# A two-layer mixture-of-experts kernel: four experts in place in layer 1, smaller first blocks, second blocks under a branch

## The chip, the cores and the metric

The kernel runs on one core of a Trainium2 chip. A core has five engines that run side by side, each through its own list of instructions in order: TensorE (PE in the profile; PEld is its weight load), VectorE (DVE), ScalarE (ACT), GpSimd (POOL) and SyncE (SP), which here only issues transfers. Sixteen DMA engines move data between HBM and the core's memory. The metric is the time of one execution in device microseconds (us); less is better.

## The reference

256 latent tokens and 256 context tokens of width 1024 pass two layers. Layer 0 mixes tokens with a bidirectional recurrence (RG-LRU), layer 1 with attention; behind each stands a mixture of experts, over all 512 tokens in layer 0 and over the 256 latent ones in layer 1. Everything is fp32. The mixture, which is what the change is about, is:

```
def grouped_moe(h, router_w, router_b, w1, w3, w2):
    logits = (h @ router_w).astype(jnp.float32) + router_b.astype(jnp.float32)
    probs = jax.nn.softmax(logits, axis=-1)
    pg = probs.reshape(probs.shape[:-1] + (N_EXPERT_GROUPS, EXPERTS_PER_GROUP))
    group_score = lax.top_k(pg, TOP_K)[0].sum(-1)
    sel = jnp.argmax(group_score, axis=-1)
    ...
    top_w, top_i = lax.top_k(masked, TOP_K)
    top_w = top_w / jnp.sum(top_w, axis=-1, keepdims=True)
    gates = jnp.sum(jax.nn.one_hot(top_i, N_EXPERTS, dtype=jnp.float32) * top_w[..., None], axis=-2).astype(h.dtype)
    y = jnp.zeros_like(h)
    for e in range(N_EXPERTS):
        y = y + gates[..., e:e + 1] * ((jax.nn.silu(h @ w1[e]) * (h @ w3[e])) @ w2[e])
    return y
```

There are 16 experts in four groups of four; each token goes to two experts of one group. `w1` and `w3` are 1024 x 512, `w2` is 512 x 1024: 2 MB each, 6 MB an expert.

How many tokens an expert gets follows from the inputs. For the inputs of these runs the counts of rows are, with the experts that stand in place by their number and the others sorted:

| | in place | by rank, from the most to the fewest |
|---|---|---|
| layer 0, both kernels | 14, 27, 62 | 183, 125, 90, 73, 73, 66, 63, 51, 47, 43, 41, 40, 26 |
| layer 1, before | 11, 25, 52 | 147, 147, 32, 29, 26, 19, 16, 7, 1, 0, 0, 0, 0 |
| layer 1, changed | 11, 25, 52, 26 | 147, 147, 32, 29, 19, 16, 7, 1, 0, 0, 0, 0 |

## The kernel before, in words

**Weights.** Every weight of the two layers passes through one pool of 2 MB tiles named `w`. A list of jobs (`moe_jobs` for the experts) gives the order; `send` takes the next job, opens a tile and issues two 1 MB halves on SP's queue (L149), with at most four halves in flight. A tile is opened when an older one is given back (`done`), so TensorE's progress releases loads.

**Places.** Experts are worked through in 16 places. The first `FIRST` = 3 places are the experts 0 to 2, fixed, so that their weights load before the router has spoken. From place 3 on a place takes the expert of a certain rank (`ORDERS`), and its weights can go out only when the counts are known: `order()` (L1017 to L1038) sorts the counts and writes the expert numbers `eok`; SP reads them with a register load (L134) and waits there. Jobs stand in the order `w1` of place e, `w3` of place e, `w2` of place e-1; only at the places named by `TAIL` does `w2` come first. In layer 1 `TAIL` is 12: the places 12 to 15 run only if they have tokens, which they have not here.

**Rooms.** A place with a rank gathers as many rows as `ROOM` says, in blocks of 128, 64 or 32 rows; 160 is 128 and 32, 96 is 64 and 32 packed. A place of the first three has 64 rows (`BASE`) and, under a branch on its count, 128 more. Rows beyond the room would go to `leftover()`, which is skipped here.

**One step** e of `run`: `ups(e)` multiplies the gathered rows by `w1` and `w3` (L935), ScalarE takes silu (L939), VectorE the product (L940), and the next place's rows are turned (`turn`, L917). Then `downs(e-1)` multiplies by `w2` (L967), VectorE scales by the gates into `y` (L978 in layer 0, L975 in layer 1), and POOL adds the rows to `yr` or to the output by a scatter transfer (L981), each waiting for the one before. Then `flips(e)` transposes what `downs(e)` will need (L947 on TensorE, copied by VectorE at L949). A branch on the number of rows stands in `ups` (L1136), in `downs` (L1152) and in the gathers (L1009), each for the engines that have work in it.

**The end of layer 0.** Layer 1 begins under layer 0's last experts: its second `qkv` tile is converted by ScalarE (`wkv`, L1320), and the low parts are taken by VectorE and POOL in turn (`wkvl`, L1321). SP reads `yr` back when all scatters are down (L1349), and the gains and residuals follow (L1356, L1359). The order of instructions on each engine is set by a scheduler when the kernel is built; a branch closes a block, and work behind it can't move ahead of it.

Of the kernel before, what the change touches and what calls it, by code (L numbers as in the profile page):

```python
# [13 lines left out]
ALU = mybir.AluOpType  # L14
# [19 lines left out]
FIRST = 3  # L34
# [14 lines left out]
C_E = 212  # L49
C_KEY = 228  # L50
C_RANK = 244
C_ROOM = 276
C_N = 308

C_LT, C_IO, C_DUP = 308, 436, 692

C_COS, C_SIN = 1076, 1204
C_ALL = 1332
# [5 lines left out]

def room(i, k):
    return MORE if k < FIRST else ROOM[i][ORDERS[i][k - FIRST]]


def blocks(i, k):

    if k < FIRST:
        return [(KIND[BASE], 0)]
    r = room(i, k)
    return [(KIND[r], 0)] if r <= 128 else [(0, 0), (KIND[r - 128], 128)]
# [3 lines left out]
def hybrid_kernel(ctx: ExitStack, tc: tile.TileContext, x, c, ctxt, c_ctx, ada_w, ada_b, norm_mix_w, norm_ffn_w,  # L78
# [39 lines left out]
    def send(pool=wp):  # L118
# [10 lines left out]
        if key[0] in ("w1", "w2", "w3") and key[2] >= FIRST:  # L129
# [65 lines left out]
    def moe_jobs(i):  # L195
        for e in range(E):
            names = [("w1", moe_w1, 0), ("w3", moe_w3, 0), ("w2", moe_w2, 1)]
            for name, w, d in names[2:] + names[:2] if e in (TAIL[i], TAIL[i] + 2) else names:
                for k in [e - d] + ([e] if d and e == E - 1 else []):
                    if 0 <= k < FIRST:  # L200
                        add_job((name, i, k), [(0, 4096, w[i, k].rearrange("(k p) f -> p k f", p=128))])
                    elif k >= FIRST:
# [522 lines left out]
    def moe_(R, rp, early):  # L725
# [17 lines left out]
        with tc.tile_pool(reuse_waits="tile", name=f"r{i}", bufs=1) as q:  # L743
            V = rp.tile([128, C, E, NV], BF16, name="V")
            cg = cst[:, C_CG:C_CG + C * E].rearrange("p (c e) -> p c e", c=C)
# [77 lines left out]
            def gates():  # L823
# [3 lines left out]
                values(0, FIRST, gate)  # L827
# [14 lines left out]
        class Lists:  # L842
# [5 lines left out]
            def match(self):  # L848
# [34 lines left out]
            def expand(self):  # L883
                m, w = self.nb, self.nb * NV
                px = mbank("pa", 1) if self.e >= FIRST or self.left else mbank("py", 2)
# [114 lines left out]
        def fetch_next(e):  # L1000
# [13 lines left out]
        def order():  # L1014

            key = rp.tile([128, E], F32, name="key")
            nc.vector.scalar_tensor_tensor(key, cnf, 16.0, cst[:, C_KEY:C_KEY + E], ALU.mult, ALU.add)  # L1017
# [48 lines left out]
        def lists(e):  # L1066
            bases = [0, BASE] if e < FIRST else [at for _, at in blocks(i, e)]
# [9 lines left out]
        def load_n(e):  # L1077
            return nc.values_load((cn if e < FIRST else counts[i][0])[0:1, e:e + 1], engines=main, min_val=0, max_val=T)
# [632 lines left out]
```

## Time and profile before

| | |
|---|---|
| three runs | 991.46, 989.19, 991.61 us; median 991.46 |
| the profiled execution | 988.14 us, of which the span of the trace is 986.1 |
| TensorE busy in the span | 860.8 us, 87%; mean granted clock 0.946 |
| VectorE, ScalarE, POOL busy | 489.9, 302.6, 252.1 us |
| moved by DMA | 277.00 MB, mean 281 GB/s |
| chain that ended last | DMA 21%, PE 11%, VectorE 6% of the span; `w` from the experts' weights 16% |

Layer 0's mixture takes about 331 to 600 us, layer 1's mixture 780 us to the end. The rows further down are from the trace of the profiled execution; their times are counted from the start of its span. L numbers are lines of the kernel before; those of the changed kernel are 10 to 15 higher (L149 becomes L159, L935 L945, L967 L977, L949 L959, L978 L988, L981 L991, L1009 L1019, L1136 L1146, L1152 L1162, L1320 L1335, L1321 L1336). In the timeline an entry in square brackets gives the idle time ahead of the instructions and what ended it.

### The profile page before, as it was taken

The page shows a single profiled execution, that of the slowest core. Times are in us where ns is not written, and L with a number is a line of the kernel's source. Part 1 is how long each engine was busy: PE and PEld are TensorE (multiplying, and loading weights), DVE is VectorE, ACT ScalarE, POOL GpSimd, SP SyncE. Part 2 cuts the span into 40 slices and gives each one's busy share as a digit, 9 for nine tenths or more (in the row PEclk, how much of TensorE's full clock was granted, in tenths as well). Part 3 has the DMA queues.
Part 4 walks back from the last instruction along what each step waited for, and adds up shares of the span by engine and source line. Part 5 has one row for each costly group of instructions (what it writes and reads, how often), then busy time and mean ns, then how long its engine had stood idle before and what let it go on. Part 6 is the DMA issues. An engine that isn't in the chain of part 4 may idle for free. (4 is left out here: it accounts for less than half of the span.)

```text
span 986.1 us, 16293 instructions
## 1 busy us (share of the span) xinstructions
PE 860.8 (87%) x6181; PEld 535.8 (54%) x6181; DVE 489.9 (50%) x1365; ACT 302.6 (31%) x554; POOL 252.1 (26%) x193
## 2 busy tenths in 40 slices
PE   3789899889996999999999984798899689999863
PEld 1356666564454655555556543587664555556541
DVE  2788797653147731321222115787861574352462
ACT  3446555674021210111111003556961221111100
POOL 2273223400002320211111114752430134132241
PEclk9799999999996999999999987899999899999985
DMA  9965974699616599999999994222939269999992
GB/s 343 352 195 189 389 275 170 245 386 387 234 71 216 206 361 382 378 365 363 363 337 353 367 348 121 79 106 74 389 127 392 104 235 377 382 374 372 368 386 73
DMA packets 126932, 277.00 MB, mean 281 GB/s; under 512 B 7976, under 2 KB 12928, under 8 KB 126832
## 3 DMA queue, kind: packets, MB, share of 16 engines
q1 hardware_dynamic: 116064, 253.77, 70.2%
q0 software_dynamic: 8896, 15.57, 6.6%
q10 hardware_dynamic: 1872, 6.37, 1.7%
q8 instruction: 58, 0.95, 0.4%
q14 instruction: 42, 0.34, 0.1%
HBM read 291.40 MB, written 15.34 MB: 311 GB/s over the span
## 5 line engine op out<-in xcount | busy, mean ns | idle before, releaser
L935 PE MATMUL up<-w,xg 128*64 128x256 f32 (+2 forms) x1600 | 168.5, 355 | 2.6 <-DMA w<-in_moe_w_dram 2.3
L967 PE MATMUL py<-w,sx 128*32 128x256 f32 (+2 forms) x720 | 133.8, 534 | 7.1 <-DMA w<-in_moe_w_dram 6.0
L935 PEld LDWEIGHTS up<-w,xg 128*64 128x64 f32 (+2 forms) x1600 | 99.5, 130 | 63.2 <-issue 31.3
L940 DVE TENSOR_TENSOR sx<-sx,up 128x256 f32<-128x256 f32 (+3 forms) x32 | 16.0, 499 | 180.8 <-PE up L935 165.0
L967 PEld LDWEIGHTS py<-w,sx 128*32 128x32 f32 (+2 forms) x720 | 47.6, 139 | 73.3 <-issue 58.7
L939 ACT ACTIVATE sx<-up 128x256 f32<-128x256 f32 (+3 forms) x32 | 12.8, 401 | 214.4 <-PE up L935 204.1
L575 POOL TENSOR_TENSOR parts<-w,parts 128x1024 fp32r<-128x1024 f32 x16 | 40.3, 2518 | 112.0 <-DVE parts L574 104.1
L935 PE MATMUL up<-w,xr 128*32 128x128 f32 (+2 forms) x640 | 61.4, 338 | 2.3 <-issue 1.6
L981 POOL DMA_INDIRECT yr<-y,yi x20 | 31.5, 1573 | 107.7 <-DVE y L978 42.8
L172 PE MATMUL bank<-hhi,parts 128*128 128x512 f32 x128 | 53.3, 416 | 4.9 <-DVE hhi L389 4.9
L521 PE MATMUL bank<-w,yT 128*128 128x512 f32 x128 | 57.3, 595 | 0.0
L173 PE MATMUL bank<-hlo,parts 128*128 128x512 f32 x128 | 52.6, 411 | 4.2 <-POOL hlo L390 2.3
L907 POOL DMA_INDIRECT xg<-hr,gi x21 | 20.8, 992 | 131.1 <-DVE f L898 62.4
L174 PE MATMUL bank<-hhi,parts 128*128 128x512 f32 x128 | 52.4, 409 | 1.3 <-POOL parts L575 1.3
L935 PEld LDWEIGHTS up<-w,xr 128*32 128x32 f32 (+2 forms) x640 | 37.1, 126 | 23.3 <-issue 16.8
L306 PE MATMUL bank<-w,st 128*32 128x512 f32 x384 | 46.5, 615 | 3.4 <-DMA w<-in_ada_w_dram 3.0
L978 DVE TENSOR_SCALAR y<-py,gt 128x512 f32<-128x512 f32 (+1 forms) x20 | 13.9, 697 | 58.9 <-PE py L967 50.6
L455 DVE TENSOR_TENSOR rt<-bank,gm 128x512 f32<-128x512 f32 x12 | 8.3, 692 | 66.9 <-PE bank L521 66.9
L922 ACT ACTIVATE xg<-tp 128x512 f32<-128x512 f32 x32 | 17.4, 594 | 77.9 <-PE tp L917 77.9
L975 DVE SCALAR_TENSOR_TENSOR xr<-py,gt,gf 32x256 f32<-32x256 f32 (+2 forms) x42 | 23.9, 570 | 28.4 <-PE py L967 14.8
L521 PEld LDWEIGHTS bank<-w,yT 128*128 128x128 f32 x128 | 23.4, 190 | 25.7 <-issue 25.5
L981 POOL DMA_INDIRECT out_dram<-xr,yi x14 | 22.2, 1584 | 58.1 <-DVE xr L975 25.1
(360 smaller groups left out, 1638.1 us busy)
## 6 DMA issues: line engine op xcount, KB each, us to landing
w<-in_moe_w_dram SPq DMA_DIRECT2D x192, 1024.0 KB
w<-in_ada_w_dram SPq DMA_DIRECT2D x48, 1024.0 KB
w<-in_lru_in_w_dram SPq DMA_DIRECT2D x8, 1024.0 KB
w<-in_attn_qkv_w_dram SPq DMA_DIRECT2D x6, 1024.0 KB
w<-in_lru_out_w_dram SPq DMA_DIRECT2D x4, 1024.0 KB
w<-in_attn_o_w_dram SPq DMA_DIRECT2D x4, 1024.0 KB
hr<-h ACTq DMA_DIRECT2D x6, 512.0 KB
yr<-zero POOLq DMA_DIRECT2D x4, 512.0 KB, 13.1
```

What stands on the lines that cost most here:

```text
L172: nc.tensor.matmul(pb, wh, xh, start=start, stop=False, skip_group_check=True)
L173: nc.tensor.matmul(pb, wh, xl, start=False, stop=False, skip_group_check=True)
L174: nc.tensor.matmul(pb, wl, xh, start=False, stop=stop, skip_group_check=True)
L306: nc.tensor.matmul(pa[32 * g:32 * g + 32, :], st[:, 4 * r + g, :], w[:, 4 * r + g, :], start=r == 0, stop=r == 1, skip_group_check=True, t ...
L521: nc.tensor.matmul(pb, src[:, k, n * 128:(n + 1) * 128], w[:, k, :], start=k == 0, stop=k == NK - 1)
L575: nc.gpsimd.tensor_sub(lo, w, h)
L907: nc.gpsimd.indirect_dma_start(out=dst[0:rows, :], out_offset=None, in_=hr[:, :], in_offset=bass.IndirectOffsetOnAxis(ap=idx[0:rows, :], a ...
L922: nc.scalar.activation(dst, pb, AF.Copy)
L935: nc.tensor.matmul(pw[g * Tn:(g + 1) * Tn, at:at + fg], hT[:, k, t0:t0 + Tn], W[:, k, g * fg:(g + 1) * fg], start=k == 0, stop=k == NK - 1 ...
L967: nc.tensor.matmul(py[j * Tn:(j + 1) * Tn, 0:wd], aT[:, ao + q * 128 + g * Tn:ao + q * 128 + (g + 1) * Tn], W2[:, f, j * dg + h * 512:j * ...
L975: nc.vector.scalar_tensor_tensor(dst[ps, :], py[ps, 0:wd], gate[ps, :], R.gf[ps, at:at + wd], ALU.mult, ALU.mult)
L981: nc.gpsimd.indirect_dma_start(out=yr[:, :].rearrange("r (g f) -> (r g) f", g=G), out_offset=bass.IndirectOffsetOnAxis(ap=ls.yi[:, z, b:b ...
```

## The change

- `FIRST` becomes a table: 3 in layer 0, 4 in layer 1. Expert 3 of layer 1 is now in place, with 64 rows and a branch for 128 more.
- The rooms change. In layer 0 the ranks 1, 2 and 3 go from 160, 128, 128 to 128, 96, 96; in layer 1 the ranks 2 and 3 go from 64 to 32. The order of ranks in layer 1 becomes 0, 2, 1, 3 from place 4 on, where it was 2, 0, 3, 1 from place 3 on.
- The ranks of `AGAIN` (1, 2, 3, 4, 6 in layer 0, which stand in the places 6, 8, 10, 12, 13; 2 and 3 in layer 1, in the places 5 and 7) get a second block of 128 rows under a branch, as the places in front have it.
- In the last place of layer 1 that surely runs (11), `downs(10)` comes before `ups(11)`, and `w2` of place 10 is loaded before `w1` and `w3` of place 11.
- The table of constants is smaller: a base column is broadcast and no longer stored 16 times.

```
-FIRST = 3
+FIRST = [3, 4]
-ORDERS = [[11, 0, 10, 1, 9, 2, 8, 3, 7, 4, 6, 5, 12], [2, 0, 3, 1, 4, 5, 6, 7, 8, 9, 10, 11, 12]]
-ROOM = [[192, 160, 128, 128, 96, 96, 64, 64, 64, 64, 64, 64, 32], [160, 160, 64, 64] + 9 * [32]]
-BASE, MORE = 64, 192
+ORDERS = [[11, 0, 10, 1, 9, 2, 8, 3, 7, 4, 6, 5, 12], [0, 2, 1, 3, 4, 5, 6, 7, 8, 9, 10, 11]]
+ROOM = [[192, 128, 96, 96, 96, 96, 64, 64, 64, 64, 64, 64, 32], [160, 160, 32] + 9 * [32]]
+AGAIN = [[1, 2, 3, 4, 6], [2, 3]]
+BASE = 64
...
+def base(i, k):
+    return BASE if k < FIRST[i] else ROOM[i][ORDERS[i][k - FIRST[i]]]
+def again(i, k):
+    return k < FIRST[i] or ORDERS[i][k - FIRST[i]] in AGAIN[i]
 def room(i, k):
-    return MORE if k < FIRST else ROOM[i][ORDERS[i][k - FIRST]]
+    return base(i, k) + 128 * again(i, k)
...
-        if key[0] in ("w1", "w2", "w3") and key[2] >= FIRST and key[1] not in counts:
+        if key[0] in ("w1", "w2", "w3") and key[2] >= FIRST[key[1]] and key[1] not in counts:
...
-            for name, w, d in names[2:] + names[:2] if e in (TAIL[i], TAIL[i] + 2) else names:
+            for name, w, d in names[2:] + names[:2] if e in (TAIL[i], TAIL[i] + 2) or e == TAIL[i] - 1 < E - 1 else names:
...
-            cg = cst[:, C_CG:C_CG + C * E].rearrange("p (c e) -> p c e", c=C)
+            cg = cst[:, C_CG:C_CG + C].unsqueeze(2).to_broadcast([128, C, E])
...
-            if e < FIRST:
-                n = nc.values_load(cn[0:1, e:e + 1], engines=[ET.Pool], min_val=0, max_val=T)
-                with tc.If(n > BASE):
+            if again(i, e):
+                n = load_n(e, [ET.Pool])
+                with tc.If(n > base(i, e)):
                     rows(128)
...
             for (kind, at), src, dst in zip(blocks(i, e), (xg[e % NX], xh), (sx[e % 2], sx[2 + e % 2])):
                 up(kind, src, W1, W3, dst)
-            if e < FIRST:
-                with tc.If(n > BASE):
+            if again(i, e):
+                with tc.If(n > base(i, e)):
                     turn(xh)
                     up(0, xh, W1, W3, sx[2 + e % 2])
                     flip(0, sx[2 + e % 2], "py")
...
-            if e < FIRST:
-                with tc.If(n > BASE):
+            if again(i, e):
+                with tc.If(n > base(i, e)):
                     down(0, sx[2 + e % 2], W2, info[e], 1, e)
...
+                last = lo == 0 and e == G - 1 < E - 1
+                if last:
+                    downs(e - 1, nb)
+                    done(("w2", i, e - 1))
...
-                if e > lo:
+                if e > lo and not last:
                     downs(e - 1, nb)
```

What becomes of it on the engines, at the places where work moves:

SP before, from layer 1's adaLN weights (`in_ada_w`) to the first load that needs the order. Each row of 128x4x512 or 128x2x1024 is a half of a tile; the rows of `in_moe_w` before `TENSOR_LOAD eok` are those of the places 0 to 2.

```order
L149 DMA w<-in_ada_w_dram 128x4x512 x4
L149 DMA w<-in_moe_w_dram 128x4x512 x8
L149 DMA w<-in_moe_w_dram 128x2x1024 x2
L149 DMA w<-in_moe_w_dram 128x4x512 x4
L149 DMA w<-in_moe_w_dram 128x2x1024 x2
L1009 UNCONDITIONAL_BRANCH
L134 TENSOR_LOAD eok
L134 ISA x2
L149 ISA
L149 DMA w<-in_moe_w_dram 128x4x512
```

SP after, the same stretch:

```order
L159 DMA w<-in_ada_w_dram 128x4x512 x4
L159 DMA w<-in_moe_w_dram 128x4x512 x8
L159 DMA w<-in_moe_w_dram 128x2x1024 x2
L159 DMA w<-in_moe_w_dram 128x4x512 x4
L159 DMA w<-in_moe_w_dram 128x2x1024 x2
L159 DMA w<-in_moe_w_dram 128x4x512 x4
L1019 UNCONDITIONAL_BRANCH
L1146 UNCONDITIONAL_BRANCH
L159 DMA w<-in_moe_w_dram 128x2x1024
L1019 UNCONDITIONAL_BRANCH
L159 DMA w<-in_moe_w_dram 128x2x1024
L144 TENSOR_LOAD eok
```

Sixteen halves of experts' weights stood ahead of the first branch (8, 2, 4 and 2); now twenty do, with the four of `w1` and `w3` of place 3 as the last. The two halves of place 2's `w2` that follow stand behind the branches of the first places.

VectorE before, the end of layer 0: `sx` are the flipped rows that the down products read (2077 of place 14, 2078 of place 15), `y` the scaled results, `wkvl` the low parts of layer 1's `qkv` tile.

```order
L949 COPY sx_2077<-pa 128x256
L949 COPY sx_2077<-pa 128x128
L940 TENSOR_TENSOR sx_2078<-sx_2078,up 128x128
L978 TENSOR_SCALAR y_2081<-py,gt 128x512
L978 TENSOR_SCALAR y_2081<-py,gt 128x256
L949 COPY sx_2078<-pa 128x128
L1321 TENSOR_TENSOR wkvl<-w,wkv 128x512
L978 TENSOR_SCALAR y_2082<-py,gt 128x256
L1321 TENSOR_TENSOR wkvl<-w,wkv 128x512 x3
```

VectorE after, from the second place-13 branch on:

```order
L1162 COMPARE_AND_BRANCH
L988 TENSOR_SCALAR y_2083<-py,gt 128x512
L1162 UNCONDITIONAL_BRANCH x2
L1336 TENSOR_TENSOR wkvl<-w,wkv 128x512 x2
L959 COPY sx_2077<-pa 128x256
L959 COPY sx_2077<-pa 128x128
L1336 TENSOR_TENSOR wkvl<-w,wkv 128x512 x2
L950 TENSOR_TENSOR sx_2078<-sx_2078,up 128x128
L988 TENSOR_SCALAR y_2081<-py,gt 128x512
L988 TENSOR_SCALAR y_2081<-py,gt 128x256
L959 COPY sx_2078<-pa 128x128
L988 TENSOR_SCALAR y_2082<-py,gt 128x256
```

The four `wkvl` stood between and behind the last `y`; now two of them stand ahead of place 14's flips and two more ahead of place 15's product (L950), behind the branch's end. ScalarE's eight conversions to `wkv` stand likewise ahead of the silu of place 15, behind which they stood before.

POOL before, the same stretch: the scatter of place 13, the two of place 14 and that of place 15, with the low parts among them.

```order
L981 DMA yr_138<-y_2082,yi 1024x512
L981 DMA yr_138<-y_2081,yi 1024x512
L981 DMA yr_138<-y_2081,yi 2048x256
L1321 TENSOR_TENSOR wkvl<-w,wkv 128x512 x2
L981 DMA yr_138<-y_2082,yi 2048x256
L1321 TENSOR_TENSOR wkvl<-w,wkv 128x512
```

POOL after:

```order
L991 DMA yr_138<-y_2082,yi 1024x512
L1162 COMPARE_AND_BRANCH
L991 DMA yr_138<-y_2083,yi 512x1024
L1162 UNCONDITIONAL_BRANCH
L1162 ISA
L1162 UNCONDITIONAL_BRANCH
L1336 TENSOR_TENSOR wkvl<-w,wkv 128x512 x4
L991 DMA yr_138<-y_2081,yi 1024x512
L991 DMA yr_138<-y_2081,yi 2048x256
L991 DMA yr_138<-y_2082,yi 2048x256
```

All four of POOL's low parts now stand between the branch of place 13 and the scatters of the places 14 and 15.

## Rows read from the trace of the kernel before

**Rows 1.** Waits, SP's queue, 330 to 600 us: total, times, longest (us).

```profile
SPq L149 <- DMA w<-in_moe_w_dram: 189.0, 75, 4.5
SPq L149 <- PEq L1136: 5.3, 2, 3.1
```

**Rows 2.** Windows: window, length, busy PE, PEld, DVE, ACT, POOL, PE clock, DMA share, GB/s.

```profile
395.00:445.00 50.00, 50.00 (x369) 26.59 (x367) 12.94 (x59) 5.70 (x12) 10.27 (x8) 1.00 1.04 369
...
579.00:600.00 21.00, 10.97 (x83) 3.76 (x83) 4.37 (x9) 4.38 (x8) 5.67 (x4) 0.81 0.64 204
```

**Rows 3.** Timeline, TensorE, end of layer 0: start, duration, line, names, shape, count, [idle before].

```profile
583.24 7.25 PE L967 MATMUL py<-w,sx 128*64 128x512 f32 x44 [2.77 <-DMA w<-in_moe_w_dram]
...
591.81 1.93 PE L967 MATMUL py<-w,sx 128*32 128x256 f32 x32 [1.06 <-DVE sx L949]
```

**Rows 4.** Timeline, VectorE, same stretch.

```profile
588.67 0.75 DVE L978 TENSOR_SCALAR y<-py,gt 128x512 f32<-128x512 f32 x1 [9.62 <-PE py L967]
...
591.67 0.68 DVE L1321 TENSOR_TENSOR wkvl<-w,wkv 128x512 fp32r<-128x512 f32 x1
```

**Rows 5.** Timeline, POOL, same stretch.

```profile
589.70 1.55 POOL L981 DMA_INDIRECT yr<-y,yi  x1 [12.97 <-DVE y L978]
595.31 1.61 POOL L981 DMA_INDIRECT yr<-y,yi  x1 [4.06 <-DVE wkvl L1321]
596.38 3.06 POOL L1321 TENSOR_TENSOR wkvl<-w,wkv 128x512 fp32r<-128x512 f32 x2
600.34 1.56 POOL L981 DMA_INDIRECT yr<-y,yi  x1 [0.91 <-DMA yr<-y,yi]
```

**Rows 6.** Timeline, SP's queue, same stretch.

```profile
606.30 0.82 SPq L1349 DMA_DIRECT2D y<-yr  x2
```

**Rows 7.** Timeline, ScalarE, same stretch.

```profile
590.89 2.19 ACT L1320 ACTIVATE wkv<-w 128x512 fp32r<-128x512 f32 x4 [13.66 <-DMA w<-in_attn_qkv_w_dram]
593.47 2.19 ACT L1320 ACTIVATE wkv<-w 128x512 fp32r<-128x512 f32 x4 [0.39 <-DMA w<-in_attn_qkv_w_dram]
```

**Rows 8.** Waits, SP's queue, 780 to 986 us.

```profile
SPq L149 <- DMA w<-in_moe_w_dram: 127.0, 55, 3.9
SPq L134 <- DVE eok L1038: 39.3, 1, 39.3
```

**Rows 9.** Windows, the stretch before the order is known.

```profile
770.00:780.00 10.00, 4.84 (x35) 3.70 (x33) 5.47 (x21) 3.76 (x7) 0.00 (x0) 0.99 0.26 104
```

**Rows 10.** Timeline, TensorE, layer 0: one 32-row up, 64-row down, 64-row up block.

```profile
433.08 3.70 PE L935 MATMUL up<-w,xh 128*32 128x128 f32 x128
...
437.79 3.65 PE L967 MATMUL py<-w,sx 128*64 128x512 f32 x16
...
442.15 7.13 PE L935 MATMUL up<-w,xg 128*64 128x256 f32 x64
```

**Rows 11.** Timeline, TensorE, layer 1, behind place 0's branch.

```profile
799.33 1.09 PE L917 MATMUL tp<-cst,xr 128*128 128x128 f32 x8 [0.77 <-DVEq L1136]
```

**Rows 12.** Timeline, TensorE, the last down products of layer 1.

```profile
964.19 1.93 PE L967 MATMUL py<-w,sx 128*32 128x256 f32 x16 [1.23 <-DMA w<-in_moe_w_dram]
...
968.75 3.64 PE L967 MATMUL py<-w,sx 128*32 128x256 f32 x32
```

**Rows 13.** Timeline, POOL, scatter-adds of layer 1.

```profile
920.10 1.57 POOL L981 DMA_INDIRECT out_dram<-xr,yi  x1 [4.54 <-DVE xr L975]
...
956.34 1.57 POOL L981 DMA_INDIRECT out_dram<-xr,yi  x1 [2.45 <-DVE r L872]
...
968.44 1.58 POOL L981 DMA_INDIRECT out_dram<-xr,yi  x1 [6.34 <-DVE xr L975]
974.89 1.58 POOL L981 DMA_INDIRECT out_dram<-xr,yi  x1 [4.88 <-DVEq L1214]
```

**Rows 14.** Chain that ended last, from 780 us: start, duration, what was waited for.

```profile
968.44 3.38 DMA out_dram<-xr,yi
```

More of the change, by code (lines that the diff above doesn't have):

```diff
@@ L48 @@
 C_CG = 148
[L49 to L58, printed above, removed]
+C_E = 152
+C_KEY = 168
+C_RANK = 200
+C_ROOM = 232
+C_N = 264
+C_LT, C_IO, C_DUP = 264, 392, 648
+C_COS, C_SIN = 1032, 1160
+C_ALL = 1288
 BLOCKS = {0: (128, [(0, 0, 0)]), 1: (64, [(1, 0, 1)]), 2: (32, [(2, 0, 2)]), 3: (96, [(1, 0, 1), (2, 64, 3)])}
 KIND = {128: 0, 64: 1, 32: 2, 96: 3}
+def base(i, k):
+    return BASE if k < FIRST[i] else ROOM[i][ORDERS[i][k - FIRST[i]]]
+def again(i, k):
+    return k < FIRST[i] or ORDERS[i][k - FIRST[i]] in AGAIN[i]
 def room(i, k):
-    return MORE if k < FIRST else ROOM[i][ORDERS[i][k - FIRST]]
+    return base(i, k) + 128 * again(i, k)
 def blocks(i, k):
-    if k < FIRST:
-        return [(KIND[BASE], 0)]
-    r = room(i, k)
+    r = base(i, k)
     return [(KIND[r], 0)] if r <= 128 else [(0, 0), (KIND[r - 128], 128)]
@@ L128, in send @@
         kw = {}
-        if key[0] in ("w1", "w2", "w3") and key[2] >= FIRST:
+        if key[0] in ("w1", "w2", "w3") and key[2] >= FIRST[key[1]]:
             i, k = key[1:]
@@ L826, in gates @@
                 nc.vector.tensor_mul(gate, pm.rearrange("p (c e) -> p c e", c=C), mx.unsqueeze(2).to_broadcast([128, C, E]))
-                values(0, FIRST, gate)
+                values(0, FIRST[i], gate)
         if i == 1:
@@ L884, in expand @@
                 m, w = self.nb, self.nb * NV
[L885 removed]
+                px = mbank("pa", 1) if self.e >= 3 or self.left else mbank("py", 2)
                 for v in range(3):
@@ L1066, in lists @@
         def lists(e):
-            bases = [0, BASE] if e < FIRST else [at for _, at in blocks(i, e)]
+            bases = [at for _, at in blocks(i, e)] + ([base(i, e)] if again(i, e) else [])
             info[e] = Lists(e, bases)
@@ L1075, in busy, with load_n @@
                 nc.tensor.transpose(pb[:, (k % 4) * 128:(k % 4) * 128 + 128], ident, ident)
-        def load_n(e):
-            return nc.values_load((cn if e < FIRST else counts[i][0])[0:1, e:e + 1], engines=main, min_val=0, max_val=T)
+        def load_n(e, engines=main):
+            return nc.values_load((cn if e < FIRST[i] else counts[i][0])[0:1, e:e + 1], engines=engines, min_val=0, max_val=T)
         def beside():
@@ L1158, in run @@
             for e in range(lo, hi + 1):
-                n1 = load_n(e + 1) if e + 1 < FIRST else None
+                n1 = load_n(e + 1) if e + 1 < hi and again(i, e + 1) else None
+                last = lo == 0 and e == G - 1 < E - 1
+                if last:
+                    downs(e - 1, nb)
+                    done(("w2", i, e - 1))
                 if e < hi:
@@ L1197, in run @@
                         info[1].index()
-                        values(FIRST, E, gp)
+                        values(FIRST[i], E, gp)
                         lists(3)
@@ L1205, in run @@
                         lists(e + 5)
-                    if FIRST <= e + 1 < hi and len(blocks(i, e + 1)) > 1:
+                    if e + 1 < hi and len(blocks(i, e + 1)) > 1:
                         turn(xh)
@@ L1276, in leftover @@
                     nk = load_n(k)
-                    if k >= FIRST:
+                    if k >= FIRST[i]:
                         eid = nc.values_load(counts[i][1][0:1, k:k + 1], engines=[ET.Pool], min_val=0, max_val=E - 1)
@@ L1673, in _constants @@
     a[:, C_E:C_E + 16] = x
-    a[:, C_KEY:C_KEY + 16] = np.where(x < FIRST, 65536 + 16384 * (FIRST - 1 - x), E - 1 - x)
     for i in range(2):
-        a[:, C_RANK + 16 * i:C_RANK + 16 * i + 16] = list(range(FIRST)) + [FIRST + r for r in ORDERS[i]]
+        k = FIRST[i]
+        a[:, C_KEY + 16 * i:C_KEY + 16 * i + 16] = np.where(x < k, 65536 + 16384 * (k - 1 - x), E - 1 - x)
+        a[:, C_RANK + 16 * i:C_RANK + 16 * i + 16] = list(range(k)) + [k + r for r in ORDERS[i]]
         a[:, C_ROOM + 16 * i:C_ROOM + 16 * i + 16] = [room(i, k) for k in range(E)]
-    a[:, C_CG:C_CG + 64] = np.repeat(128 * np.arange(4) - FAR, 16)
+    a[:, C_CG:C_CG + 4] = 128 * np.arange(4) - FAR
     return a
```

10 lines of the change are left out of this document (5 added, 5 removed).

## The prediction

> **What bounds the kernel now.** I read the page first, then the waits of SP's queue in both mixtures of experts, then the timeline around the two places where the order of work changes.
>
> In layer 0's mixture the loads bound. Of SP's waits from 330 to 600 us, 189.0 us in 75 waits are for an earlier load to land; the largest wait for TensorE is 5.3 us [rows 1]. From 395 to 445 us the DMA engines are full (share 1.04, 369 GB/s) and TensorE is busy too (50.00 of 50) [rows 2]: the stage is nearly balanced, but TensorE is the one that ends up waiting: the last down products of the layer wait 2.77 us for `w` [rows 3]. Then a serial tail follows: down products of place 14 (583.24) [rows 3], `y` on VectorE (588.67) [rows 4], three scatter-adds one behind another at 589.70, 595.31, 600.34 [rows 5], and the read of `yr` on SP at 606.30 [rows 6], on which all of layer 1 depends. Beside this tail ScalarE converts the next `qkv` tile, whose halves it can use at 590.89 and 593.47 [rows 7].
>
> In layer 1's mixture the loads bound again, but with a hole before them: SP sits 39.3 us for the experts' order, later 127.0 us in 55 waits for loads [rows 8]. The hole is nearly empty: the DMA engines' share is 0.26 from 770 to 780 us [rows 9]. What is loaded in the hole is free.
>
> **Part A, the end of layer 0 (a loss).** The place-13 branch is new (rank 6), and its last block closes late. The order shown with the change has the `qkv` conversions ahead of the flips, `y` and scatters of places 14 and 15; before, they stood between and behind these. VectorE executes in order, so its two `wkvl` now hold the copies (flips) of place 14, without which TensorE cannot begin downs(14); ScalarE's eight conversions stand ahead of silu(15) in the same way, and POOL's four `wkvl` ahead of the last three scatters. All wait for the `qkv` load. That load can hardly come sooner, since it stands behind the same number of loads on a queue that loads bound [rows 1, 2].
>
> Steps: first half usable 590.89; ScalarE needs 2.19/4 = 0.55 us a conversion [rows 7], so the third ends near 592.5; VectorE's `wkvl` takes 0.68 [rows 4], so its second ends near 593.2; two copies of about 0.35 each (an estimate between the `y` rows' 0.48 and nothing) give 593.9. Downs(14) begin there instead of a little before 583.24. TensorE has then idled for some 15 us. After the 2.77 us of idling in the kernel before, with a granted clock of 0.81 over that stretch [rows 2], 44 products took 7.25 us, and `y` came 588.67 - 583.24 = 5.43 us after their start, behind 12 of the 64-row part's 16 products (of 16 + 32 in all, four were done earlier) [rows 3, 4]. [...] The scatter follows 589.70 - 588.67 = 1.03 later: 600.3 to 601.2 for 589.70, that is +10.6 to +11.5. POOL's four `wkvl` at 3.06/2 [rows 5] run from about 592 and end by 598.5: not last. The scatters keep their spacings (5.61, 5.03) and the read of `yr` its 5.96 behind the last [rows 5, 6]. **+11**; with TensorE at full speed +8.5; at worst +12.5 if the second half's conversions also count.
>
> **Products of layer 0 (nothing).** Place 6 goes from 160 to 128 rows: a 32-row up block costs 3.70 us [rows 10], its downs 1.93 [rows 3], with turn and flip 6.9. Places 8 and 10 go from 128 to 96. A 64-row up block is 7.13, its down 3.65 [rows 10], a 32-row pair 5.63: taking 128 rows as two of 64 and 96 as 64 and 32, each saves 10.78 - 5.63 = 5.15. Sum -17.2. Five new branches take back 5 x (0.77 + 0.16), about 5, the up branch by its row [rows 11], the down branch by an estimate of a fifth of it. The rest, -12, is hidden: the loads set the stage's end [rows 1], and part A now waits for a load in any case. If the cover were gone it would be worth those 12 us.
>
> **Part B, the start of layer 1's mixture (a gain).** With four experts in place, `w1` and `w3` of place 3 go out before the order is known: 20 halves instead of 16 stand ahead of the SP's wait. They use the two tiles that the output projection has given back, in the hole of rows 9. The loads after the hole are then 26 tiles instead of 28. Their price: from the first load's issue at 797.62 (where the 39.3 us wait of rows 8 ends, plus the register load) to the landing that TensorE waits for until 964.19 [rows 12], 27 tiles: 166.6/27 = 6.17 us each. Two are 12.3 us. Against it, the next load now needs TensorE past the first branch, 799.33 [rows 11]: +1.7. The loads end 10.6 us earlier.
>
> Does the end follow? The three last scatters start at 956.34, 968.44 and 974.89 [rows 13]; the span ends 986.1. The swap puts downs(10) ahead of ups(11), and the load of place 10's `w2` ahead of `w1`, `w3` of place 11, so that the last two scatters stand as far apart as before or farther, while the last `w2` is the last load either way: I cost the swap itself at nothing, hidden under the last loads; without that cover it shifts one scatter by 1.93 + 3.64 [rows 12]. The scatter of place 6 at 920.10 [rows 13] is set by TensorE, which saves only place 5's 64 to 32 rows, 7.13 + 3.65 - 3.70 - 1.93 = 5.15, and pays about 2.5 for three more branches. The scatters behind it, some 8 to 9 us each while loads run, thus come about 3 earlier; the one at 956.34 near 953. Its landing is the next limit: the next scatter follows in up to 968.44 - 956.34 = 12.1 us while loads run, and an undisturbed one lands within 3.38 [rows 14]. I take 7.5 for the one and 4 for the other, so that the last scatter starts at about 965 in place of 974.89: **-9.6**, with -11.5 if the loads alone decide and -5 if the scatters do.
>
> **Small parts.** A smaller constants table, a base column broadcast, counts loaded by POOL alone: each is off the path; zero to 0.5 either way. The counts that follow from the inputs fill no second block: the ranks given one (layer 0: 125, 90, 73, 73, 63 rows; layer 1: 32, 29) lie within their rooms, so every new block is skipped.
>
> **Sum.** 986.1 + 11 - 9.6 = 987.5 of span, 1.4 more. The profiled run took 988.14, the median of three 991.46; on the median: 991.46 + 1.4 = **992.9**. One measurement of this kernel can tell about 0.3%, 3 us, from no change.
>
> **Rivals.**
> 1. *Slower: the scatters of layer 1 are the bound.* Place 6's second scatter is set by TensorE; three new branches could eat the 5.15 us saved, and each later scatter waits for the one before. Then the scatter at 956.34 does not move, and only the last two gain: 1 to 6 us, taken as 4. 11 - 4 = +7: 998.5. For it: spacings of 12.1 and 6.45 in rows 13. Against: the 12.1 us are mostly a wait for `w`, as TensorE's row at 964.19 [rows 12] shows. It decides from where that scatter starts over 5 us later than the loads allow. Chance 0.22.
> 2. *Faster: the late tail of layer 0 runs less loaded.* The three scatters now fall after 600 us, when fewer loads run; if each takes the 3.38 us of rows 14 instead of 5 to 6, part A is about +5: 986.9. Against: the third (600.34) took 5.96 to the read with loads already few [rows 5, 6]. Chance 0.13.
> 3. *Faster: the hold-up is hidden*, because `qkv` lands some 10 us earlier or the order on the engines proves harmless. Only B stays: 981.9. Against: rows 1. Chance 0.06.
> 4. *TensorE bounds layer 0 after all*, and its -12 counts: 981. For it: 50.00 of 50 busy [rows 2]. Against: the waits for `w` [rows 3]. Chance 0.03.
> 5. *Branches dear.* A skipped up branch held TensorE 0.77 us [rows 11]. If none of the eight new places hides its pair of 0.77 + 0.16, B is less by 3 x 0.93 = 2.8 and A more by the one that stands in it, about 1: 996.7. Chance 0.05. [...]
> 6. *The change does not do what it says*: a second block runs. One 128-row block is about twice a 64-row one, 2 x (7.13 + 3.65) = 21.6 us, at least 1010 in layer 1. Against: the counts. Chance 0.01.
>
> **Chances.** The forecast has 0.50, from 988 to 999 by its bounds taken together (A 8.5 to 12.5, B -5 to -11.5). Faster by over 3 us: rivals 2 to 4 in most of their spread and a little of the forecast, 0.20. Slower by over 3 us: rivals 1, 5, 6 and a part of the forecast, 0.33. Within: 0.47. For 8 in 10 the range leaves out rivals 3, 4 and 6 and the far ends of 1 and 2: 985 to 1000.
>
> **What would show it.** Part A right: the last down products of layer 0 start at 593 to 595 us, the read of `yr` at 616 to 618; wrong if they start before 585. Part B right: 20 halves of experts out before the hole, and, measured from the read of `yr`, the last scatter 9 to 10 us sooner. Rival 1 shows as POOL waiting for its own earlier scatter, with no wait for `w` in the last 30 us on TensorE. I am wrong outright if the difference sits elsewhere, in layer 0's stage before 579 us or in attention.

## The result

The changed kernel takes 1014.27 us (median of four runs, 1012.56 to 1015.41), the kernel before 990.33 beside it: the ratio is 1.0242, with a 95% interval of 1.0216 to 1.0267. It is slower by 24 us. The forecast was 992.9, from 985 to 1000.

The profiled execution has a span of 1013.7 us for 986.1, so +27.6. The table follows it through four marks to the end; each is the same point of the work in both traces.

| mark | before | after | shift | added since the mark above |
|---|---|---|---|---|
| first up product of layer 0 | 323.76 | 325.53 | +1.8 | +1.8 |
| read of `yr` (end of layer 0) | 606.30 | 619.52 | +13.2 | +11.4 |
| first up product of layer 1 | 791.44 | 808.13 | +16.7 | +3.5 |
| down products of place 6 done | 920.83 | 949.88 | +29.1 | +12.4 |
| end of the span | 986.1 | 1013.7 | +27.6 | -1.5 |

The +1.8 at the first mark is no work of the change: over all fifteen traces this product starts at 322.7 to 326.4 us. So part A came near its forecast, and part B, which should have taken 9.6 us away, is not to be seen: layer 1's mixture became longer.

**The end of layer 0, after.** The timeline of TensorE, ScalarE, VectorE, POOL and SP's queue, in this order (start, duration, line, names, shape, count, [idle before]); the rows answer to [rows 3 to 7].

```profile
580.56 1.94 PE L945 MATMUL up<-w,xg 128*32 128x128 f32 x32 [2.69 <-DMA w<-in_moe_w_dram]
596.94 8.26 PE L977 MATMUL py<-w,sx 128*64 128x512 f32 x48 [14.45 <-DVE sx L959]
```

```profile
593.50 2.19 ACT L1335 ACTIVATE wkv<-w 128x512 fp32r<-128x512 f32 x4 [25.99 <-DMA w<-in_attn_qkv_w_dram]
```

```profile
594.16 0.69 DVE L1336 TENSOR_TENSOR wkvl<-w,wkv 128x512 fp32r<-128x512 f32 x1 [22.48 <-ACT wkv L1335]
...
596.47 0.61 DVE L959 COPY sx<-pa 128x256 f32<-128x256 f32 x2
...
603.39 0.75 DVE L988 TENSOR_SCALAR y<-py,gt 128x512 f32<-128x512 f32 x1 [3.29 <-PE py L977]
```

```profile
594.74 6.29 POOL L1336 TENSOR_TENSOR wkvl<-w,wkv 128x512 fp32r<-128x512 f32 x4 [21.23 <-ACT wkv L1335]
604.41 1.56 POOL L991 DMA_INDIRECT yr<-y,yi  x1 [3.39 <-DVE y L988]
```

```profile
619.52 0.82 SPq L1364 DMA_DIRECT2D y<-yr  x2
```

TensorE's last up products begin at 580.56, and then it has nothing it may do. ScalarE sits 25.99 us for the `qkv` load, VectorE 22.48 us for ScalarE's conversion, and only behind VectorE's two `wkvl` come the copies (596.47) that TensorE's down products wait 14.45 us for (596.94). POOL's low parts (594.74) are in their place ahead of the scatters, but not last. All 48 down products take 8.26 us, with a granted clock of 0.66 from 596.94 to 605.20; `y` follows at 603.39 for 588.67, the scatter stands at 604.41 for 589.70, the read of `yr` at 619.52 for 606.30.

**Layer 1's mixture, after.** Windows of TensorE by place: first the kernel before, then the changed one (window, length, busy PE, PEld, VectorE, ScalarE, POOL, granted clock, DMA share, GB/s). The stretches are: up products of place 0 to those of place 3; place 3; place 4 to place 6; place 6 to place 8.

```profile
791.44:829.66 38.22, 33.52 (x282) 21.01 (x282) 25.39 (x117) 7.03 (x17) 11.88 (x11) 1.00 0.86 310
829.66:842.81 13.15, 12.99 (x106) 7.83 (x104) 6.74 (x24) 2.08 (x6) 5.48 (x5) 1.00 1.04 369
842.81:883.87 41.06, 41.06 (x331) 22.73 (x330) 15.76 (x54) 5.78 (x16) 10.46 (x9) 1.00 1.04 379
883.87:921.13 37.26, 37.13 (x387) 20.85 (x385) 14.78 (x54) 5.49 (x15) 8.03 (x7) 1.00 1.05 376
```

```profile
808.13:849.52 41.39, 36.46 (x285) 22.70 (x286) 26.18 (x117) 7.29 (x18) 11.85 (x11) 0.92 0.85 310
849.52:865.52 16.00, 13.34 (x109) 8.07 (x107) 8.56 (x28) 2.17 (x6) 7.08 (x6) 0.99 1.04 367
865.52:910.57 45.05, 41.31 (x393) 22.70 (x393) 14.19 (x50) 5.58 (x16) 8.83 (x8) 0.93 0.99 354
910.57:950.17 39.60, 36.60 (x402) 21.67 (x400) 14.78 (x56) 5.49 (x15) 8.00 (x7) 0.96 0.89 313
```

Before, TensorE is busy 41.06 of 41.06 and 37.13 of 37.26 us. It has no slack there, although the loads are full as well (share 1.04 and 1.05). After, each stretch is longer (41.39, 16.00, 45.05, 39.60 for 38.22, 13.15, 41.06, 37.26), the busy time is longer in three of them and only 0.5 us shorter in the fourth, and the clock is lower in all of them (0.92, 0.99, 0.93, 0.96 for 1.00), although place 5's smaller block takes 5.15 us of products out. TensorE's waits from place 0 to place 8, before and after (total, times, longest):

```profile
PE tp L917 <- DVEq L1136: 2.6, 3, 1.2
PE pa L887 <- DVE r L872: 1.8, 2, 1.5
```

```profile
PE tp L927 <- DVEq L1146: 4.3, 6, 1.2
PE py L957 <- DVEq L1162: 3.1, 2, 2.2
PE pa L897 <- issue: 2.2, 1, 2.2
PE tp L927 <- DMA xh<-hr,gi: 1.8, 1, 1.8
```

All rows of these two answers sum to 5.5 and 14.8 us; nothing in either is a wait for weights. The new ones stand at the branches (L1146 and L1162) and at the gather of the second rows (`xh`); for 2.2 us the trace shows no releaser (`issue`). Among and behind them stand products at a lower granted clock, 0.56, 0.90 and 0.84 over these three groups:

```profile
829.02 6.41 PE L977 MATMUL py<-w,sx 128*64 128x512 f32 x16
...
865.52 15.50 PE L945 MATMUL up<-w,xr 128*128 128x512 f32 x32
```

```profile
898.84 10.67 PE L977 MATMUL py<-w,sx 128*128 128x512 f32 x48
```

The same three groups took 3.65, 13.90 and 8.98 us before, at 1.00. With 0.63 at place 7 (4.89 us at 0.74 for 4.26 at 1.00) this is 6.7 us. Waits +9.3, clock +6.7, products -5.15: 10.9 of the 12.4 us; the rest is in no single row.

SP's queue from 790 us on answers to [rows 8]:

```profile
SPq L159 <- DMA w<-in_moe_w_dram: 94.5, 43, 3.7
SPq L159 <- PEq L1146: 37.5, 4, 27.5
SPq L159 <- PE up L945: 21.8, 4, 13.2
```

127.0 us of waiting for loads became 94.5. Of the 37.5 us at branches 27.5 are one wait at the first branch, in the hole where SP sat 39.3 us for the order before. What is new behind it are the 21.8 us for up products, with the longest, 13.2 us, between 910 and 950 us: there the queue waits for TensorE.

### The profile page after: what moved, and what is told of

It reads as the page before. It is cut to its first block, busy times and chain, and to the rows that moved or that the text cites. A ratio compares the mean times of both kernels' runs of the same rounds, so it can differ in the third digit from the quotient of the medians.

```text
span 1013.7 us, 17132 instructions
## 1 busy us (share of the span) xinstructions
PE 854.2 (84%) x6495; PEld 538.8 (53%) x6495; DVE 488.6 (48%) x1366; ACT 299.5 (30%) x549; POOL 252.4 (25%) x193
## 3 DMA queue, kind: packets, MB, share of 16 engines
q8 instruction: 64, 1.05, 0.4%
## 5 line engine op out<-in xcount | busy, mean ns | idle before, releaser
L945 PE MATMUL up<-w,xg 128*32 128x128 f32 (+2 forms) x1984 | 161.4, 338 | 10.1 <-DMA w<-in_moe_w_dram 9.4
L977 PE MATMUL py<-w,sx 128*32 128x256 f32 (+2 forms) x768 | 130.1, 521 | 19.1 <-DVE sx L959 17.9
L945 PEld LDWEIGHTS up<-w,xg 128*32 128x32 f32 (+2 forms) x1984 | 104.6, 127 | 60.4 <-issue 24.3
L950 DVE TENSOR_TENSOR sx<-sx,up 128x256 f32<-128x256 f32 (+3 forms) x31 | 13.4, 434 | 176.0 <-PE up L945 94.1
```

The lines of the kernel that those rows point to most:

```text
L945: nc.tensor.matmul(pw[g * Tn:(g + 1) * Tn, at:at + fg], hT[:, k, t0:t0 + Tn], W[:, k, g * fg:(g + 1) * fg], start=k == 0, stop=k == NK - 1 ...
L977: nc.tensor.matmul(py[j * Tn:(j + 1) * Tn, 0:wd], aT[:, ao + q * 128 + g * Tn:ao + q * 128 + (g + 1) * Tn], W2[:, f, j * dg + h * 512:j * ...
```

## The experiments

Theory 1 is the hold-up of part A. Theory 2 says that TensorE paces layer 1's mixture and that each branch there costs it a wait and then slower products. Theory 3 says that layer 1's loads then run ahead, so that part B is worth little. All times are medians beside runs of the kernel before, at 989.4 to 990.1 us.

| run | us | against |
|---|---|---|
| late_conv | 999.76 | changed kernel 1014.27: -14.5 |
| no_again_l0 | 993.69 | changed kernel: -20.6 |
| no_again_l1 | 1003.57 | changed kernel: -10.7 |
| no_again | 984.58 | changed kernel: -29.7; before: ratio 0.9946 (0.9929 to 0.9963) |
| no_branch_place3 | 984.20 | no_again: -0.4 |
| three_in_place | 986.62 | no_again: +2.0 |
| no_swap | 983.38 | no_again: -1.2 |
| old_rooms_l0 | 990.57 | no_again: +6.0 |
| branches_8_9 | 991.01 | no_again: +6.4 |
| branches_early_l0 | 994.73 | no_again: +10.2 |
| best | 978.60 | before: ratio 0.9894 (0.9878 to 0.9910) |
| best_old_rooms | 982.40 | best: +3.8 |
| best_three_in_place | 986.61 | best: +8.0 |

**late_conv: the conversions behind layer 0's last scatter, branches kept.**

```
             one = nc.scalar.activation(hi[:, k, :], w, AF.Copy)
             low.tensor_sub(lo[:, k, :], w, hi[:, k, :])
+            if key == ("qkv", 2):
+                tc.add_manual_dep(one.ins, state["tail"].ins.name, mybir.DependencyInfo(
+                    mybir.DependencyClass.NoSync, mybir.DependencyReason.SCHED_ONLY), reason="behind layer 0")
```

`state["tail"]` is the last scatter-add that `down` has issued.

> The changed kernel with one edit: the eight conversions of layer 1's second qkv tile on ScalarE may only be placed behind layer 0's last scatter-add (an order for the scheduler, no wait). All branches stay. Theory 1 (the hold-up at the end of layer 0 is only that these conversions stand ahead of the last places' work): layer 0's last down products start at about 584 to 587 us instead of 596.9, the read of yr is issued at 606 to 609 instead of 619.5, and the whole time falls by 11 to 13 us, from 1014 to 1001 to 1003. Rival (the new branches themselves make layer 0 longer, and the conversions only fill the idle time): the read of yr stays at 615 or later and the time falls by under 4 us. Layer 1 should not change under either.

The fall is 14.5 us. TensorE's last down products and SP's read, in its timeline:

```profile
582.89 6.60 PE L977 MATMUL py<-w,sx 128*64 128x512 f32 x44 [0.49 <-DMA w<-in_moe_w_dram]
```

```profile
605.68 0.82 SPq L1367 DMA_DIRECT2D y<-yr  x2
```

582.89 and 605.68 are the times of the kernel before (583.24, 606.30). The five branches are still there, so it is the order of the conversions that makes part A, as read from the built order. The size is a little more than expected. From layer 0's first up product to the read of `yr` it is 283.0 us here and 294.0 in the changed kernel, so 11.0. Layer 1's mixture, which this edit leaves as it was, is shorter in this trace too, 199.0 us for 205.6; the profiled run, 995.28 us, is 4.5 under the median of its four.

**no_again_l0: no second blocks in layer 0.** `AGAIN = [[], [2, 3]]`

> The changed kernel without the five second blocks under a branch in layer 0 (rooms and all of layer 1 as changed). Theory 1: as with the conversions put behind, the read of yr comes at 605 to 607 us and the time falls by 12 to 14 us, to about 1001; the difference to that run, 0 to 2 us, is what the five branches cost by themselves under the loads. Rival (rooms that are smaller help once TensorE is free of branches): the read of yr comes before 600 us, and the time falls by 18 or more.

-20.6 is more than the 12 to 14 expected and in the rival's range, though the read of `yr` comes at 605.37, within theory 1's. Against late_conv 6 us remain. In the traces 3.3 us stand in layer 0's mixture (279.7 us from its first up product to the read of `yr`, 283.0 in late_conv), where the five branches differ and the place of the conversions. More stands behind: from the read of `yr` to layer 1's first up product it is 184.5 us here, 188.9 in late_conv, 185.1 in the kernel before and 188.6 in the changed one. In the three traces with all five branches this stretch is 188.1 to 188.9 us, in the twelve others 184.1 to 187.6, on the mean 185.8: some 3 us, with a spread as large. ScalarE's conversions of the next `qkv` tile (`wq`) are mixed differently with the attention's work in the two orders. That this mixing costs the 3 us is argued from the order; no run isolates it.

**no_again_l1: no second blocks in layer 1.** `AGAIN = [[1, 2, 3, 4, 6], []]`

> The changed kernel without the two second blocks under a branch in layer 1 (places 5 and 7); place 3 in place keeps its branch, layer 0 as changed. Theory 2 (layer 1's mixture is paced by TensorE, and each branch costs it a wait and then slower products at the lower clock): from place 4's first up product to place 8's first the stretch shrinks from 84.6 us to about 76 (5 to 12 us), and the whole time by 5 to 11 us, to 1003 to 1009. Rival (branches cost their 0.9 us each, and what makes layer 1 longer is the place-3 expert in place and the order of loads): under 2.5 us.

-10.7 us. From place 4 to place 8:

```profile
866.88:907.14 40.26, 39.21 (x394) 22.12 (x393) 13.60 (x50) 5.40 (x16) 8.81 (x8) 0.96 0.98 351
907.14:942.18 35.04, 35.03 (x402) 20.59 (x401) 14.77 (x56) 5.47 (x15) 8.02 (x7) 1.00 0.99 342
```

40.26 + 35.04 = 75.3 us for 84.65: 9.35 us for two branches whose blocks never run, 4.7 each. TensorE's waits in this stretch fall to 1.1 us in all, and the clock is 0.96 and 1.00 instead of 0.93 and 0.96. The rival is out. Of theory 2 the waits stand, but not the slower products: late_conv has both branches and the same waits here, 6.3 us, at the full clock:

```profile
851.17:892.47 41.30, 38.00 (x395) 21.61 (x393) 14.35 (x50) 5.67 (x16) 8.85 (x9) 1.00 1.03 368
892.47:930.72 38.25, 35.26 (x402) 20.57 (x400) 14.77 (x56) 5.47 (x15) 7.99 (x7) 1.00 0.96 334
```

That is 79.55 us; no_again_l0, the third trace with both branches, has 81.88. Against 75.3 us the pair of branches so costs 4.3, 6.6 and 9.35 us. About 5 us of it, the waits, are in all three; the slower products come and go.

**no_again: neither.** `AGAIN = [[], []]`

> The changed kernel without any of the seven second blocks under a branch: what is left is four experts in place in layer 1, the smaller rooms, the order of ranks, and the swap in place 11. Theories 1 and 2 together: the two falls add up, 13 + 8 = 21 us, to about 993, with 988 to 998. If both were shadows of one cause, the sum is less than the two apart by over 4 us. The kernel before stands at 990.3.

-29.7 us for 20.6 + 10.7 = 31.3: they add within 1.6 us. Layer 1's two branches are worth 10.7 us beside those of layer 0 and 993.69 - 984.58 = 9.1 without them. Below the expected 988, and 0.54% faster than the kernel before. So the other edits are a gain, and the seven branches made all of the loss.

**no_branch_place3, three_in_place, no_swap, old_rooms_l0**, each one edit from no_again, shown in this order (of no_swap two pieces, in the loads and in `run`). three_in_place also gets a 13th rank in layer 1's order and rooms, so that the expert with 26 rows has 32 rows of room there, and 64 in place.

```
-    return k < FIRST[i] or ORDERS[i][k - FIRST[i]] in AGAIN[i]
+    return k < 3 or k >= FIRST[i] and ORDERS[i][k - FIRST[i]] in AGAIN[i]
...
-FIRST = [3, 4]
+FIRST = [3, 3]
...
-    ... or e == TAIL[i] - 1 < E - 1 else names
+    ... else names
-                last = lo == 0 and e == G - 1 < E - 1
+                last = False
...
-ROOM = [[192, 128, 96, 96, 96, 96,
+ROOM = [[192, 160, 128, 128, 96, 96,
```

> The changed kernel without any second block under a branch (as the run before this batch, median 984.6) and, besides, without the branch of layer 1's place 3: its expert stays in place with 64 rows, and rows beyond these would go to the leftover path. Theory 2 (TensorE paces layer 1's mixture up to place 6, and a branch costs it 2 to 4 us there): the stretch from place 3's first up product to place 4's first shrinks from 16.7 us to 13.1 to 14, and the whole time by 2 to 4 us, to 980.5 to 982.5. Rival (at this place the branch is hidden, since the rows for the next place or loads are late anyway): under 1 us.

The stretch from place 3's up products to place 4's is 13.16 us (830.48 to 843.64), for 16.69 in no_again, as expected, but the time falls by 0.4 only. Where the median loses the 3.5 us these two traces do not show: behind place 8 they differ by 0.8 us (62.56 here, 61.75 in no_again). What the swap does at the end shows against `best`, which differs from this run by the swap alone and takes 57.21 us behind place 8. POOL's last three scatters, first in this run, then in `best`:

```profile
953.52 1.58 POOL L991 DMA_INDIRECT out_dram<-xr,yi  x1 [3.58 <-DMA out_dram<-xr,yi]
958.74 1.55 POOL L991 DMA_INDIRECT out_dram<-xr,yi  x1 [3.64 <-DMA out_dram<-xr,yi]
...
968.73 1.59 POOL L991 DMA_INDIRECT out_dram<-xr,yi  x1 [6.22 <-DVEq L1229]
```

```profile
955.50 1.58 POOL L991 DMA_INDIRECT out_dram<-xr,yi  x1 [3.80 <-DVE r L901]
...
960.42 1.58 POOL L991 DMA_INDIRECT out_dram<-xr,yi  x1 [1.12 <-DVE f L908]
965.75 1.57 POOL L991 DMA_INDIRECT out_dram<-xr,yi  x1 [3.75 <-issue]
```

With the swap the last two stand 9.99 us apart, without it 5.33: place 11's up products stand behind place 10's down products (954.63 here, 950.42 in `best`), and place 11's whole chain hangs on the end.

> As the run without any second block under a branch, but with three experts in place in layer 1 again (order of ranks 0, 2, 1, 3, 4 and so on from place 3 on; small rooms and swap kept). It takes away part B of the prediction and the branch of place 3. My part B (loads bound): slower by 8 to 10 us, to 993 to 995, and TensorE waits for weights in the last 30 us. Theory 3 (TensorE paces the stage to about 920 us and scatters behind, the loads run ahead of it by 10 us): the time moves by -3 to +3 us, 982 to 988, with waits for weights of at most 5 us.

+2.0, inside theory 3's range. I took that as the worth of part B. It was the wrong reading. This run has the swap and no branch at place 3, so it stands against no_branch_place3: +2.4 us. Without the swap the same step is 8.0 (best_three_in_place): the swap hid the rest.

> As the run without any second block under a branch, but place 11 of layer 1 in the old order: up products of place 11 before the down products of place 10, loads of w1 and w3 of place 11 before w2 of place 10. If the swap is hidden under the last loads and scatters, as costed in the prediction: within 1.5 us of 984.6. If it keeps the last scatters apart and so pays: slower by 2 to 5 us. If it puts place 10's copies and y ahead of place 11's products on VectorE and so costs: faster by 2 to 4 us.

-1.2 us, inside "hidden". Beside place 3's branch the swap indeed costs next to nothing; without that branch it costs 984.2 - 978.6 = 5.6, and with three in place 986.62 - 986.61, nothing. Why the branch covers it is not shown.

> As the run without any second block under a branch, but with layer 0's rooms of before (160, 128 and 128 rows for the ranks 1 to 3). It puts back some 17 us of TensorE's products in layer 0. The prediction's step (the loads set that stage's end): within 1 us of 984.6, TensorE busy 15 to 17 us longer, and the read of yr again at 605 to 607 us. Rival (TensorE bounds layer 0's mixture): slower by 8 us or more, the read of yr at 614 or later.

+6.0: neither is right. TensorE is busy 254.2 us from 330 to 590 for 244.3, so 10 more and not 15 to 17; the read of `yr` is at 605.87, and from the first up product to it there are 282.4 us for 280.3, so 2.0 us more. best_old_rooms takes up the other 4.

**branches_8_9.** `AGAIN = [[], [4, 5]]`

> The changed kernel with second blocks under a branch nowhere but at the ranks 4 and 5 of layer 1, which stand in the places 8 and 9, behind the two 160-row places. It moves the two branches of layer 1 out of the stretch that TensorE paces. At the places 5 and 7 the two cost 9 to 11 us. Theory 2 in the sharp form (a branch costs only where TensorE has no slack; behind place 7 TensorE waits 8 us for scatters anyway): 0 to 3 us more than 984.6. Rival (each branch costs 4 to 5 us wherever it stands): 992 to 995.

+6.4, 3.2 each: in between, so the sharp form of theory 2 falls. At place 9 TensorE, which waited 8.39 us in no_again, now waits longer, and with the turn of the next rows still undone:

```profile
944.62 1.94 PE L927 MATMUL tp<-cst,xr 128*128 128x128 f32 x8 [10.77 <-DVEq L1146]
```

```profile
945.17 0.22 PE L897 MATMUL pa<-r,dup_b 128*128 128x5 bf16 x3 [8.39 <-DVE r L882]
```

At the branch TensorE waits for VectorE; work that slipped into a wait (the turn, 1.09 us at 935.68 in no_again) now stands behind it. TensorE's slack at this place did not cover that.

**branches_early_l0.** `AGAIN = [[1, 2, 3], []]`

> The changed kernel with second blocks under a branch only at the ranks 1, 2 and 3 of layer 0 (places 6, 8, 10), none in layer 1. The last branch is now five places before the end of layer 0, yet in the order built from it three of VectorE's and three of POOL's low parts of the qkv tile still stand ahead of place 14's results and scatters. Theory 1 as read from the order: place 14's first scatter goes out at 597 to 599 us, 7 to 9 later than 589.7, the read of yr at 611 to 614, and the time is 6 to 9 us over 984.6. Rival (only a branch in the last places holds the block back; branches under the loads are free): within 1.5 us of 984.6 and the read of yr at 604 to 606.

The rows come as read from the order, POOL first, then SP:

```profile
591.27 4.61 POOL L1336 TENSOR_TENSOR wkvl<-w,wkv 128x512 fp32r<-128x512 f32 x3 [20.47 <-ACT wkv L1335]
596.03 1.82 POOL L991 DMA_INDIRECT yr<-y,yi  x1 [0.16 <-issue]
```

```profile
612.46 0.82 SPq L1364 DMA_DIRECT2D y<-yr  x2
```

596.03 for an expected 597 to 599, 612.46 for 611 to 614; the time is +10.2 (6 to 9 expected), in a run that spreads from 988.8 to 1001.0. A branch five places before the end still changes where the conversions are put.

**best: no_again without place 3's branch and without the swap.**

> A version meant to beat both: the changed kernel without any second block under a branch in either layer beyond the places 0 to 2, with the place order 11 of before (no swap). Small rooms and four experts in place stay. From the single runs, 984.2 without place 3's branch and 983.4 without the swap against 984.6: 982 to 984 if the two gains of 0.4 and 1.2 add, 984 to 986 if they were noise. In any case under the kernel before by 4 to 8 us.

978.60 us, 1.1% under the kernel before, and 6.0 under no_again, for 0.4 and 1.2 when each was tested alone: each of the two hid what the other cost.

**best_old_rooms and best_three_in_place**, one edit each from `best` (as above).

> The fastest version so far (no second blocks under a branch beyond the places 0 to 2, no swap; 978.6) with layer 0's rooms of before. In the earlier pair the old rooms cost 6.0 us, of which the traces place 2.0 in layer 0 (from the first up product to the read of yr: 280.3 against 282.4) and the rest behind it, where nothing differs. If the rooms are worth what the order shows (POOL's low parts stand between the last two scatters with the old rooms, behind all of them with the small ones): 1 to 3 us, 980 to 982. If the 6 us are real and repeat: 983 to 986; then from first up product to read of yr must show 4 or more, or TensorE's granted clock behind it must be lower by as much.

+3.8, though the intervals of the two ratios still overlap (0.9901 to 0.9956; 0.9878 to 0.9910). From the first up product of layer 0 to the read of `yr` there are 281.8 us for 280.0. That much repeats: the three traces with old rooms have 281.8 to 282.5, the eight with small rooms and no branches in layer 0 have 279.0 to 280.5. POOL's low parts, which stand between the last scatters in the order, do not make it. The first of the three scatters already starts 265.2 us after the first up product (588.41), in `best` 263.0 (588.38). Ahead of it TensorE's last large group of down products takes longer, here first, then in `best`:

```profile
581.95 7.60 PE L977 MATMUL py<-w,sx 128*64 128x512 f32 x44 [2.41 <-DMA w<-in_moe_w_dram]
```

```profile
583.78 5.39 PE L977 MATMUL py<-w,sx 128*64 128x512 f32 x44 [0.50 <-DMA w<-in_moe_w_dram]
```

The other 2 us lie behind the read of `yr`, above all in the gaps of layer 1's last scatters (7.13 us for 4.92 between the third and second last), where both kernels run the same list. Why is open.

> The fastest version so far (978.6) with three experts in place in layer 1 instead of four: part B of the prediction alone, with neither a branch nor the swap beside it. Prediction's part B (loads bound the stage): slower by 8 to 11 us, 987 to 990. Theory 3 (TensorE and the scatters pace it, the loads run ahead): 979 to 983, that is 0 to 4 us.

+8.0 us: the lower end of what was expected of part B, and twice the end of theory 3's range. It is a net figure, since the expert with 26 rows has 5.15 us of products less with three in place. TensorE waits for weights again, five times from 950 to 962 us; three of them:

```profile
950.33 1.08 PE L945 MATMUL up<-w,xg 128*32 128x128 f32 x32 [1.85 <-DMA w<-in_moe_w_dram]
953.04 1.62 PE L945 MATMUL up<-w,xg 128*32 128x128 f32 x32 [1.63 <-DMA w<-in_moe_w_dram]
...
961.46 1.94 PE L977 MATMUL py<-w,sx 128*32 128x256 f32 x16 [0.67 <-DMA w<-in_moe_w_dram]
```

In `best` no such wait is left. So theory 3 falls in this form: the loads do set the end, once branches, swap and scatters no longer do.

## Why the prediction was wrong

**Part A was right.** Mechanism and place are shown by late_conv and branches_early_l0. The forecast was +11; the trace shows +13.2 at the read of `yr`, of which 1.8 were there before the mixture began, so 11.4; against late_conv it is 11.0. That the number fits so well is in part luck. Its scatter at 600.3 to 601.2 has `y` 5.4 to 6.3 us behind the start of the last down products at 593.9, an estimate that no run here shows behind such a hold-up. In the changed kernel it was 6.45 us (596.94 to 603.39), at a granted clock of 0.66. Both signs named for it were missed by 1.5 to 2 us (596.94 for "593 to 595", 619.52 for "616 to 618"), since the `qkv` half was usable at 593.50 for 590.89. The first scatter came 14.7 us later, where 10.6 to 11.5 were forecast, and the scatters behind it then stood closer: 15.1 us from the first to the read of `yr`, for the 16.6 kept in the forecast.

**Part B: the loads were sized right, what stands beside them was not.** With nothing else in the way four in place are worth 8.0 us (best_three_in_place) for the 9.6 of the forecast, within its bounds of 5 to 11.5. The step that failed is "pays about 2.5 for three more branches": the two at places 5 and 7 cost 4.3 to 9.35 us in three traces and 9.1 to 10.7 in the medians, and the stretch at place 3 is 3.5 us shorter without its branch. The prediction priced a branch by one wait, 0.77 us [rows 11]. It left out that a branch also makes later reads of the same stretch wait (2.23 and 2.16 us at the flips and index products, both gone in no_again_l1), and that the gather of the next rows then waits too (1.85 us at place 4, gone in `best`). Products at a lower clock (10.67 us at 0.84 for 8.98 at 1.00) came on top in the changed kernel's trace; late_conv, with the same branches, has 8.98. And it let these 2.5 be set against a saving of 5.15, on an engine that had no slack in that stretch: 41.06 busy of 41.06. I read TensorE's few waits for `w` at 958 to 964 us as "the loads bound again", when from place 4 to place 8 TensorE was as full as the loads.

**The swap "at nothing" was wrong too,** but only where the end is free: 1.2 us beside place 3's branch, 5.6 without it. The cover that the step named was the last loads. Where TensorE still waits for these, with three in place, the swap costs nothing (986.62 and 986.61); with four in place no such wait is left in `best`.

**Layer 0's products "nothing":** small rooms are worth 3.8 to 6.0 us in the median. Some 2 us of it are shown in layer 0, ahead of the last scatters, so the loads did not hide all of the products; the rest is open.

**Behind layer 0**, 3.5 us between the read of `yr` and layer 1's mixture had no step in the prediction at all; against the mean of the traces without the five branches it is 3. Their cause is open.

**The rivals.** Rival 5 (branches dear) was the right kind of miss, at 996.7 and 0.05: its price per branch was 0.93 us, the measured one 3.2 to 5.4 in the medians of pairs (6.4, 9.1 and 10.7 us for two). What the changed kernel's trace shows at the branches, from place 0 to place 8, is that TensorE waits for VectorE: 4.3 us in six waits at L1146 and 3.1 us in two at L1162. For the 2.16 us ahead of the index products, right behind place 5's branch, it shows no releaser. Rival 1 (scatters) describes the end of no_again. Rival 2 happened in a small part, the 1.5 us by which the scatters stood closer, and so did rival 4, in the 2 us of layer 0. Rival 3 did not happen. The measured time is where rival 6 put it ("at least 1010"), but no second block ran: TensorE is busy 854.2 us in all, for 860.8 before.

## What to carry to other kernels

Where two resources are both full (here TensorE busy 41.06 of 41.06 us beside a DMA share of 1.04), a shorter load queue is worth only what the other leaves: read the busy share of the pacing engine in each stretch, not the last wait. A block that is skipped is not free; price its branch by all the waits that go when it goes, about 2.5 us each here and not one of 0.77, and look in the built order for what the scheduler moved across it, at the ends of stages above all. When edits are tested one by one, test them from the version in which the others are gone: part B read as 2 us beside the swap and as 8 without it. And before a part of a difference is given a cause, look at other traces with the same list: the stretch from place 4 to place 8 took 79.6, 81.9 and 84.7 us with the same two branches.

## What was not expected of the hardware

Two skipped branches took 9.35 us of TensorE's time, and only 5.7 of it is idle: from place 4 to place 8 the waits fall from 6.8 to 1.1 us when the branches go. The other 3.7 us are slower products (77.9 us busy for 74.2); the granted clock of the two stretches rises from 0.93 and 0.96 to 0.96 and 1.00. These 3.7 us are no fixed price of the pauses. late_conv has the same branches and pauses, none over 2.3 us in either trace, and a clock of 1.00 in both stretches. What lowered the clock in the one execution and not in the other is not shown.
